# Last third of a down projection by seven products for six of eight blocks, up tiles woven three deep, and adding transfers issued later

## The chip, the cores and the metric

The kernel runs on one core of a Trainium2 chip. The metric is the device time of one execution in microseconds (us): the median of three runs. A further execution was recorded by the hardware profiler; its instruction times, waits and transfers are the trace that the text reads.

## What is computed

One inference step of a hybrid decoder layer for a prompt of 512 tokens and 8 sample tokens with shared weights: mixer, cross attention and a gated feed-forward part, each added to the residual. All numbers are 32-bit floats. The change touches the feed-forward part alone:

```python
def conv_ffn(xn, prefix, w_up, conv_w, conv_b, w_down):
    T = xn.shape[1]
    up = xn @ w_up                                   # 1024 -> 2 x 2816
    ext = jnp.concatenate([prefix, up], axis=1)
    c = conv_b
    for k in range(CONV_W):                          # width 3, causal
        c = c + conv_w[k] * ext[:, k:k + T]
    gate, val = jnp.split(c, 2, axis=-1)
    return (jax.nn.silu(gate) * val) @ w_down, ext[:, -(CONV_W - 1):]
...
    y_ffn, ffn_state = conv_ffn(rmsnorm(h, g_ffn), ffn_prefix, w_up, conv_w, conv_b, w_down)
    return h + y_ffn, pool_state, nsa_state, ffn_state
```

A final rmsnorm over the 1024 channels of `h + y_ffn` follows.

## The kernel before

Channels lie on the 128 partitions, the 520 tokens in two halves `r` of 260 columns (`HT`). There are `KT` = 8 blocks of 128 model channels and `FT` = 22 tiles of 128 hidden channels; an up tile `j` has a gate and a value part (`v` = 0, 1). For precision a weight block W is split into a rounded part `w_hi` (ScalarE copy, L117) and the rest `w_lo` (VectorE subtraction, L120), the moving operand likewise, and a product of two blocks takes three matmuls: hi by hi, hi by lo and lo by hi. A matmul has 260 columns. So one classic block of weights costs six matmuls for both token halves.

**Seven products.** Up tiles `NA` = 7 to 21 go by a Strassen-Winograd scheme (`up_seven`): the gate and value parts against the even and odd blocks of input channels form a 2 by 2 block product with the two token halves, which takes seven half-token products of 4 x 3 = 12 matmuls instead of eight. They are named 1, 5, 2, 6, 3, 7, 4 in the code. Products 1, 6, 7 and 4 go into one half `a` of a PSUM bank, 5 and 3 into its other half `c`, product 2 into a bank `b`. Product 7 adds onto what 6 left in `a`, so `a` has to be read between them. The mixed inputs (`xm4`, `xm3`) are made once by `mixes`. The mixed weights are made per tile: products 5 and 7 need a sum of two blocks of `w_up`, which a DMA from GpSimd's queue adds in memory to a block that has been loaded (L1880, `accum_op`); product 6 needs the block of 1 plus that of 5 (`sum2`) and product 3 the block of 2 plus that sum (`sum4`), which VectorE adds (L120, `tt`).

**The down projection** sums over 22 hidden tiles in three parts (`PARTS`: tiles 0-6, 7-14, 15-21). Each part runs over the 8 output blocks `d`; each group is added to the residual `hT` (L120). Parts 0 and 1 are woven between the up products (`downs`), part 2 comes last: blocks 0 to 3 as steps (`last_down`), blocks 4 to 7 in the tail (L2070), one token half after the other, so that the norm and the stores of half 0 (L2030, L2048, L2052) can run beside half 1.

**The order of the work.** `steps` is a list of steps, each one load (SyncE's queue, `load_unit`), one split (`prep`), the matmuls (`mm`, L1829 for classic, L1890 for the seven) and what follows them (`post`). The loop over `m` issues the load up to `EARLY` = 13 steps ahead, the split `AHEAD` = 3 steps ahead, then the matmuls of step `m`, then `POPS` = 2 pieces of the deferred convolution and gate work (`behind`: `conv`, L1680 to L1684, and `gate`). Loads go to 13 units of raw weights (`w_u`, `raw_x`); splits to a ring of four units (`w_hi`, `w_lo`). A unit is loaded again when the splits and sums that read it are done. A list scheduler of the framework then orders each engine's queue. Every engine works its queue in order. From tile 8 on, a row of the steady pattern is: seven steps of 12 matmuls and one `downs` block of 42 or 48.

Of the kernel before, what the change touches and what calls it, by code (L numbers as in the profile page):

```python
# [9 lines left out]
F32 = mybir.dt.float32  # L10
# [22 lines left out]
FT = DFF // P  # L33
MEM = 256
# [73 lines left out]
def decoder_step(ctx: ExitStack, tc: tile.TileContext, A, O):  # L108
# [1580 lines left out]
    def gate(j):  # L1689
# [6 lines left out]
        yield  # L1696
        tt(g, g, u, OP.mult)
        yield
        if NA <= j < PARTS[2][0]:
            if not hid_mid:  # L1700
                hid_mid.extend(ptile(ab3, [P, KT, 2, HT], t, F32R, name="h_mid") for t in ("x3_hi", "x3_lo"))
            hid[j] = tuple(t[:, j - NA] for t in hid_mid)
        else:
            hid[j] = tuple(ptile(ff, [P, 2, HT], t, F32R, bufs=7) for t in ("h_hi", "h_lo"))
# [25 lines left out]
    NI = KT // 2  # L1730
    xm4 = [ptile(actp, [P, 4, NI, HT], "act_a", F32R, bufs=2, name="xm4") for _ in range(2)]
    xm3 = ptile(ff, [P, 2, 3, NI, HT], "xm3", F32R)
    B11, B21, B22, T3_, N1, N2, T4_ = range(7)
# [25 lines left out]

    mix = mixes()  # L1760
# [28 lines left out]
    class Step:  # L1789

        def __init__(self, mm, load=None, prep=None, post=None, held=False):
            self.load_, self.prep_, self.mm_, self.post_, self.held = load, prep, mm, post, held
# [23 lines left out]

    def classic(ps_of, src, xs, kt, post):

        out = []
        for k0 in range(0, kt, 4):  # L1820
# [11 lines left out]
            out.append(Step(mm, load=lambda k0=k0, n=n: load_unit(rows(src, k0, n), n), post=post if k0 + n == kt else None))  # L1832
# [12 lines left out]
    def up_classic(j):  # L1845
        out = []
        for v in range(2):
# [8 lines left out]
            out.append(classic(ps, w_up[:, up_cols(v, j)], xs3, KT, post))  # L1856
        return out[0] + out[1]

    def down(pi, d, then=None):
# [8 lines left out]
        return classic(ps, w_down[j0 * P:j1 * P, d * P:(d + 1) * P], lambda k: hid[j0 + k], j1 - j0, post)  # L1868

    def up_seven(j):  # L1870

        ac, bb = held("pp"), held("t")

        def block(m, s):
            return w_up[:, up_cols(m, j)].rearrange("(i s p) c -> p s i c", s=2, p=P)[:, s]

        def both(a, b):
            def load():
                u = load_unit(a)
                pool.dma_start(u[1], b, accum_op=OP.add)  # L1880
# [33 lines left out]

        def out21():
            acopy(exts[j][:, 1, 0, 2:], a_of(False), scale=-1.0)
            behind.extend((conv(j, 1), gate(j)))

        s = {}
        s[1] = Step(product(a_of, B11, True), lambda: load_unit(block(0, 0)), held=True)  # L1920
        s[5] = Step(product(c_of, N1, True), both(block(1, 0), block(1, 1)), post=keep, held=True)
        s[2] = Step(product(b_of, B21, True), lambda: load_unit(block(0, 1)), post=out11, held=True)

        def sum2():
            tt(s[1].raw, s[1].raw, s[5].raw, OP.add)
            s[5].free()
            return s[1].raw

        def sum4():
# [244 lines left out]
```

## Time and profile before

| | |
|---|---|
| median of three runs (lowest, highest) | 827.56 us (827.38, 827.99) |
| the profiled execution, by its own time | 827.17 us |
| its span, first to last instruction | 825.5 us |
| mean granted TensorE clock | 0.996 |
| TensorE, VectorE, ScalarE busy share of the span | 98%, 73%, 54% |
| last loads, splits and matmuls of the up and down stage with seven products | 509 to 815 us of the span |

The profile's lines give busy time, count and mean duration of a group; matmuls overlap, so the mean duration of one (285 ns) is longer than the distance from one to the next (about 120 ns), which the chain of waits shows. In the chain, PE is TensorE. DVE is VectorE, ACT ScalarE, POOL GpSimd, SPq SyncE's queue.

### The profile page before, as it was taken

The page shows a single profiled execution, that of the slowest core. Times are in us where ns is not written, and L with a number is a line of the kernel's source. Part 1 is how long each engine was busy: PE and PEld are TensorE (multiplying, and loading weights), DVE is VectorE, ACT ScalarE, POOL GpSimd, SP SyncE. Part 2 cuts the span into 40 slices and gives each one's busy share as a digit, 9 for nine tenths or more (in the row PEclk, how much of TensorE's full clock was granted, in tenths as well). Part 3 has the DMA queues.
Part 4 walks back from the last instruction along what each step waited for, and adds up shares of the span by engine and source line. Part 5 has one row for each costly group of instructions (what it writes and reads, how often), then busy time and mean ns, then how long its engine had stood idle before and what let it go on. Part 6 is the DMA issues. An engine that isn't in the chain of part 4 may idle for free.

```text
span 825.5 us, 17791 instructions
## 1 busy us (share of the span) xinstructions
PE 808.3 (98%) x6891; PEld 753.7 (91%) x6891; DVE 605.2 (73%) x1460; ACT 447.9 (54%) x940; POOL 95.3 (12%) x100
## 2 busy tenths in 40 slices
PE   9999999899999999999999999999999999999996
PEld 8998878877778899999799999999999999999995
DVE  6644686887657776888673799997888887887714
ACT  6741347667665553444343465666666656665541
POOL 2300111000000031000032000111111111100021
PEclk9999999999999999999999999999999999999998
DMA  9988975833222283677443224756866866754422
GB/s 327 304 257 289 411 285 182 270 115 116 77 77 53 64 254 106 202 251 254 137 115 103 77 78 126 154 134 152 165 143 147 168 145 142 160 135 121 171 110 104
DMA packets 146366, 137.87 MB, mean 167 GB/s; under 512 B 6417, under 2 KB 133265, under 8 KB 144089
## 3 DMA queue, kind: packets, MB, share of 16 engines
q1 hardware_dynamic: 127224, 114.63, 44.5%
q0 software_dynamic: 18624, 21.26, 12.0%
q8 instruction: 54, 0.88, 0.4%
q10 hardware_dynamic: 432, 0.84, 0.3%
q14 instruction: 32, 0.25, 0.1%
HBM read 129.56 MB, written 10.69 MB: 170 GB/s over the span
## 4 chain that ended last, share of the span: by engine, by line
PE 90%; DVE 3%; ACT 3%; DMA 2%; issue 1%; SPq 0%; DVEq 0%; ACTq 0%
PE ps_pp L205 29%; PE ps_pp L1890 16%; PE ps_pp L1829 16%; PE ps_t L1890 3%; PE ps_tb L1266 3%; PE ps_o L1155 2%; PE ps_pp L2070 2%; PE ps_tb L1072 2%; PE ps_sc L1108 2%; PE ps_tf L1140 2%; PE ps_x L1467 1%; PE ps_tb L1234 1%; PE ps_x L1488 1%; ACT prob L1118 1%; PE ps_s L1528 1%
## 5 line engine op out<-in xcount | busy, mean ns | idle before, releaser
L1890 PE MATMUL ps_pp<-xm,w_hi 128*128 128x260 f32 x720 | 133.3, 285 | 0.0
L1890 PEld LDWEIGHTS ps_pp<-xm,w_hi 128*128 128x128 f32 x720 | 110.9, 188 | 2.3 <-ACT ext L117 0.2
L117 ACT ACTIVATE w_hi<-w_u 128x512 fp32r<-128x512 f32 (+2 forms) x110 | 72.7, 661 | 66.4 <-PE ps_pp L1890 22.7
L1890 PE MATMUL ps_pp<-xm,w_lo 128*128 128x260 f32 x360 | 101.5, 282 | 0.0
L120 DVE TENSOR_TENSOR w_lo<-w_u,w_hi 128x512 fp32r<-128x512 f32 (+2 forms) x110 | 80.1, 729 | 16.6 <-ACT w_hi L117 15.3
L1890 PEld LDWEIGHTS ps_pp<-xm,w_lo 128*128 128x128 f32 x360 | 67.7, 188 | 0.0
L120 DVE TENSOR_TENSOR hT<-hT,ps_pp 128x520 f32<-128x520 f32 (+1 forms) x44 | 28.4, 645 | 45.0 <-PE ps_pp L205 17.9
L205 PE MATMUL ps_pp<-x_hi,w_hi 128*128 128x260 f32 x288 | 59.9, 286 | 0.0
L205 PE MATMUL ps_pp<-x_hi,w_lo 128*128 128x260 f32 x288 | 59.6, 285 | 0.0
L205 PE MATMUL ps_pp<-x_lo,w_hi 128*128 128x260 f32 x288 | 58.5, 284 | 0.0
L117 ACT ACTIVATE w_hi<-w_raw 128x1024 fp32r<-128x1024 f32 (+1 forms) x38 | 35.1, 922 | 41.3 <-PE ps_pp L205 30.0
L1118 ACT ACTIVATE prob<-prob,mx 128x384 f32<-128x384 f32 (+3 forms) x64 | 35.4, 555 | 19.3 <-DVE mx L1116 19.1
L120 DVE TENSOR_TENSOR w_lo<-w_raw,w_hi 128x1024 fp32r<-128x1024 f32 (+1 forms) x38 | 41.4, 1089 | 6.1 <-ACT w_hi L117 5.8
L205 PEld LDWEIGHTS ps_pp<-x_hi,w_lo 128*128 128x128 f32 x288 | 44.9, 188 | 0.6 <-issue 0.4
L205 PE MATMUL ps_pp<-xn_hi,w_hi 128*128 128x260 f32 x208 | 45.1, 291 | 0.2 <-issue 0.2
L205 PEld LDWEIGHTS ps_pp<-x_hi,w_hi 128*128 128x128 f32 x288 | 44.9, 188 | 0.3
L1880 POOL DMA_DIRECT2D w_u<-in_w_up_dram x19 | 24.4, 1286 | 178.9 <-DMA w_u<-in_w_up_dram 106.8
L205 PEld LDWEIGHTS ps_pp<-x_lo,w_hi 128*128 128x128 f32 x288 | 44.4, 188 | 0.4 <-issue 0.4
L120 DVE TENSOR_TENSOR w_lo<-raw_x,w_hi 128x512 fp32r<-128x512 f32 (+1 forms) x53 | 35.7, 674 | 10.3 <-ACT w_hi L117 9.6
L205 PE MATMUL ps_pp<-xn_lo,w_hi 128*128 128x260 f32 x208 | 42.9, 285 | 0.3 <-DVE xn_lo L129 0.3
L205 PE MATMUL ps_pp<-xn_hi,w_lo 128*128 128x260 f32 x208 | 43.0, 286 | 0.0
L117 ACT ACTIVATE w_hi<-raw_x 128x512 fp32r<-128x512 f32 (+1 forms) x53 | 32.8, 618 | 18.1 <-PE ps_pp L1890 13.1
(495 smaller groups left out, 2309.8 us busy)
## 6 DMA issues: line engine op xcount, KB each, us to landing
w_u<-in_w_up_dram SPq DMA_DIRECT2D x57, 256.0 KB, 3.2
xkr<-in_cache_mem_dram SPq DMA_DIRECT2D x16, 512.0 KB, 4.7
xvr<-in_cache_mem_dram SPq DMA_DIRECT2D x16, 512.0 KB, 7.1
raw_x<-in_w_up_dram SPq DMA_DIRECT2D x26, 256.0 KB, 3.4
Kt<-in_k_t_dram SPq DMA_DIRECT2D x48, 128.0 KB, 3.2
w_u<-in_w_up_dram SPq DMA_DIRECT2D x10, 512.0 KB, 4.3
w_u<-in_w_down_dram SPq DMA_DIRECT2D x20, 256.0 KB, 4.4
w_u<-in_w_up_dram POOLq DMA_DIRECT2D x19, 256.0 KB, 5.8
```

Of the source, the lines that this page charges most:

```text
L117: act.activation(o, i, AF.Copy, scale=scale)
L120: (eng or dve).tensor_tensor(o, a, b, op=op)
L205: pe.matmul(o, a[:, k, :], x[:, hf, :], start=(k == 0 and j == 0), stop=(k == kt - 1 and j == 2))
L1072: pe.matmul(ps[:, :HT], a[:, k, :], y[x][:, k, hf, :], start=(k + j == 0), stop=(k == 3 and j == 2))
L1108: pe.matmul(ss_[hl][:, 0:n], Qst[:, h, qc], k[:, g, u, 0:n], start=(u == 0), stop=(u == 1), skip_group_check=True)
L1118: act.activation(p[:, 0:nk], p[:, 0:nk], AF.Exp, bias=mx[:, hh:hh + 1], scale=-1.0, accum_out=sm[:, hh:hh + 1])
L1140: pe.transpose(pt[:, hh * P:(hh + 1) * P], pr[hh][:, kb * P:(kb + 1) * P], ident)
L1155: pe.matmul(po[hp * 64:(hp + 1) * 64, g * 256:(g + 1) * 256], Vtok[:, br, kb, g * 64:(g + 1) * 64], pTs[kb][:, hp * 256:(hp + 1) * 256], s ...
L1266: pe.matmul(ps[i], x[:, k, ts_], w[:, kl, :], start=(k == 0 and j == 0), stop=(k == KT - 1 and j == 2))
L1829: pe.matmul(ps[:, hf, :HT], a[:, k, :], x[:, hf, :], start=(k0 + k + j == 0), stop=(k0 + k == kt - 1 and j == 2))
L1880: pool.dma_start(u[1], b, accum_op=OP.add)
L1890: pe.matmul(ps, a[:, i, :], b, start=(first and i + q == 0), stop=(i == NI - 1 and q == 2), skip_group_check=True)
```

## The change

1. **Part 2 of the down projection by seven products.** `PARTS` becomes tiles 0-6, 7-13 and 14-21, so the last part has eight hidden tiles. `DOWN_ORDER` puts its even tiles ahead of its odd ones. Output blocks 0 to 5 go in three pairs through `down_seven`; blocks 6 and 7 stay classic in the tail (`D0` = 6). The gated values of tiles 14 to 21 are kept unsplit (`raw_hid`) and `hidden_mixes` makes the mixed and split operands from them (`hx_b`, `hx_m`, `hx_e`) while the last five `downs` blocks run. Sums of weights for these three groups are made by VectorE.
2. **Up tiles woven three deep** (`weave`): a row is 6 of tile s, 1 of t, 4 of the tile before s, 3 of s, a `downs` block in rows 0 to 7 alone, 5 and 2 of t, 7 of s. Rows 8 to 13 have no `downs` block; the last row takes three. `sum2` and `sum4` of tiles 8 to 21 become adding DMAs from one raw unit to another on GpSimd's queue (`dma`), issued right after the splits of products 5 and 2.
3. **Adding transfers later:** the adding DMAs of products 5 and 7 are issued `LATER` = 5 steps after their load, or when their split comes within four steps, not with the load. What is read of `a` and `c` after product 2 now includes the copy that followed product 5 before (`out11`). Posts get high priority; `POPS` is 3.
4. **Layouts:** `w_up` and `w_down` are laid out so that a partition's part of a block lies in one row of 2 KB (before: rows of 512 bytes).
5. **Tail:** the weights of blocks 6 and 7 are split beside the last four steps, and the norm and stores of half 0 stand at fixed places of half 1 (`lead`, `issue_after`).

```diff
@@
+PARTS = ((0, 7), (7, 14), (14, FT))
+DOWN_ORDER = list(range(14)) + list(range(14, FT, 2)) + list(range(15, FT, 2))
...
+        if j >= NB2:
+            if not raw_hid:
+                raw_hid.append(ptile(ff, [P, KT, 2, HT], "hA", name="raw_hid"))
+            tt(raw_hid[0][:, j - NB2], g, u, OP.mult)
...
+    def hidden_mixes():
...
+        for i in range(NI):
+            e, o = raw_hid[0][:, 2 * i], raw_hid[0][:, 2 * i + 1]
+            both = raw_hid[0][:, 2 * i:2 * i + 2].rearrange("p s r t -> p r s t")
+            at_ = [t[:, :, i].rearrange("p (r s) t -> p r s t", r=2) for t in blk]
+            acopy(at_[0], both)
+            n, t = (ptile(ff, [P, 2, HT], "cv", bufs=3, name="hz") for _ in range(2))
+            tt(n[:, 0], e[:, 0], e[:, 1], OP.subtract)
+            tt(t[:, 0], o[:, 1], e[:, 1], OP.subtract)
+            dve.scalar_tensor_tensor(n[:, 1], n[:, 0], -1.0, o[:, 1], op0=OP.mult, op1=OP.subtract)
+            acopy(mid[:, 0, 2, i], t[:, 0])
+            dve.scalar_tensor_tensor(t[:, 1], n[:, 1], -1.0, o[:, 0], op0=OP.mult, op1=OP.subtract)
+            acopy(mid[:, 0, 0:2, i], n)
+            tt(at_[1], both, at_[0].bitcast(F32), OP.subtract)
+            acopy(end[:, 0, i], t[:, 1])
+            tt(mid[:, 1, 0:2, i], n, mid[:, 0, 0:2, i].bitcast(F32), OP.subtract)
+            tt(mid[:, 1, 2, i], t[:, 0], mid[:, 0, 2, i].bitcast(F32), OP.subtract)
+            tt(end[:, 1, i], t[:, 1], end[:, 0, i].bitcast(F32), OP.subtract)
...
+    LATER = 5
+    adds = []
+
+    def seven(block, mixed, ac, bb, posts, dma):
...
                 u = load_unit(a)
-                pool.dma_start(u[1], b, accum_op=OP.add)
+                adds.append([LATER, u[1], b])
...
+        def add(o, a):
+            if dma:
+                pool.dma_start(s[o].raw, s[a].raw, accum_op=OP.add)
+            else:
+                tt(s[o].raw, s[o].raw, s[a].raw, OP.add)
 
         def sum2():
-            tt(s[1].raw, s[1].raw, s[5].raw, OP.add)
             s[5].free()
             return s[1].raw
 
         def sum4():
-            tt(s[2].raw, s[2].raw, s[1].raw, OP.add)
...
+    def weave(rows, places, last):
+        prev = None
+        for n, s in enumerate(rows):
+            t = rows[n + 1] if n + 1 < len(rows) else None
+            seq = ([s[6], t[1]] if prev and t else [t[1], s[6]] if t else [s[6]]) + ([prev[4]] if prev else [])
+            if t:
+                seq += [s[3]] + (downs.pop(0) if n in places else []) + [t[5], t[2], s[7]]
+            else:
+                seq += last() + [s[3]] + last() + [s[7]] + last() + [s[4]]
+            steps.extend(seq)
+            prev = s
+
+    weave(sevens, (0, 1, 2, 3, 4, 5, 6, 7), lambda: downs.pop(0))
...
-    D0 = 4
-    for d in range(D0):
-        steps += last_down(d)
+    D0 = 6
+    groups = [down_seven(q, down_done) for q in range(D0 // 2)]
+    steps += [groups[0][i] for i in (1, 5, 2)]
+    weave(groups, (), lambda: [])
...
-    AHEAD, EARLY, POPS = 3, 13, 2
+    AHEAD, EARLY, POPS = 3, 13, 3
...
+        soon = [s.raw for s in steps[max(m + AHEAD, 0):m + AHEAD + 4] if hasattr(s, "raw")]
+        for e in list(adds):
+            e[0] -= 1
+            if e[0] <= 0 or any(e[1] is r for r in soon):
+                adds.remove(e)
+                pool.dma_start(e[1], e[2], accum_op=OP.add)
```

Where sums of weights are made shows in the queues. In these rows `w_u` and `raw_x` are raw units, `in_w_up` is the matrix in memory. GpSimd's queue before, five rows of the steady pattern:

```order
L1880 DMA w_u_5885<-in_w_up_dram 128x4x128 [waits DMAHW5_49,DMASW1_49]
L1880 DMA raw_x_5483<-in_w_up_dram 128x4x128 [waits DMAHW3_49,DMASW2_49,DVE_49]
L1880 DMA w_u_5884<-in_w_up_dram 128x4x128 [waits DMAHW4_49,DMASW3_49]
L1880 DMA w_u_5885<-in_w_up_dram 128x4x128 [waits DMAHW2_49,DMASW4_49,DVE_49]
L1880 DMA w_u_5885<-in_w_up_dram 128x4x128 [waits DMAHW3_49,DMASW5_49]
```

Each row adds a block from memory to a loaded unit, two per tile, and nothing else stands between them.

GpSimd's queue in the changed kernel, tiles 19 to 21 in the rows without a `downs` block:

```order
L1966 DMA raw_x_5483<-raw_x_5483 128x512 [waits DVE_49,Activation_49]
L1966 DMA raw_x_5483<-raw_x_5483 128x512 [waits DMASW4_49,DMAHW6_49,DMASW3_49,DVE_49]
L2115 DMA raw_x_5483<-in_w_up_t_dram 128x512 [waits DMAHW4_49,DMASW5_49]
L1966 DMA w_u_5885<-w_u_5885 128x512 [waits DMASW6_49,DVE_49,Activation_49]
L1966 DMA w_u_5885<-w_u_5885 128x512 [waits DMAHW3_49,DMASW6_49,DVE_49]
L2115 DMA w_u_5885<-in_w_up_t_dram 128x512 [waits DMAHW3_49,DMASW0_49]
L1966 DMA w_u_5884<-w_u_5884 128x512 [waits DMASW2_49,DMASW1_49,DMAHW1_49,DVE_49,Activation_49]
L1966 DMA raw_x_5483<-w_u_5884 128x512 [waits DMAHW0_49,DMASW1_49,DVE_49]
```

The adds of loaded blocks (L2115, L1880 before) stay; each tile gains a pair of adds from unit to unit (L1966), the second of which waits for the first to land.

VectorE's queue before, around the two sums of one tile (`w_lo` rows are splits, the rows with two raw units are `sum4` and `sum2`):

```order
L120 TENSOR_TENSOR raw_x_5483<-raw_x_5483,w_u_5885 128x512
L120 TENSOR_TENSOR hT_2321<-hT_2321,ps_pp_7482 128x520 [waits PE_49]
L120 TENSOR_TENSOR w_lo_5889<-w_u_5885,w_hi_5888 128x512 [waits DMAHW2_49,Activation_49]
L1913 SCALAR_TENSOR_TENSOR ext0_5890<-ps_pp_7372,ext0_5890 128x260 [waits PE_49]
L120 TENSOR_TENSOR w_lo_5887<-w_u_5885,w_hi_5886 128x512 [waits DMAHW3_49,Activation_49]
L120 TENSOR_TENSOR w_u_5885<-w_u_5885,raw_x_5483 128x512 [waits DVE_49]
```

Each sum stands just ahead of the split that reads it, or one or two places earlier, in the same queue.

VectorE's queue in the changed kernel, a row without a `downs` block; the five rows are the splits of 4 (tile 18), 3 (tile 19), 5 and 2 (tile 20) and 7 (tile 19):

```order
L122 TENSOR_TENSOR w_lo_5887<-w_u_5885,w_hi_5886 128x512 [waits DMAHW0_49,Activation_49]
L122 TENSOR_TENSOR w_lo_5887<-raw_x_5483,w_hi_5886 128x512 [waits DMASW4_49,Activation_49]
L122 TENSOR_TENSOR w_lo_5889<-w_u_5885,w_hi_5888 128x512 [waits DMASW6_49,PE_49,Activation_49]
L122 TENSOR_TENSOR w_lo_5889<-w_u_5885,w_hi_5888 128x512 [waits DVE_49,DMAHW3_49,PE_49,Activation_49]
L122 TENSOR_TENSOR w_lo_5887<-w_u_5884,w_hi_5886 128x512 [waits DMASW1_49,PE_49,Activation_49]
```

The sums are gone from VectorE's queue; the split of 3 now waits for a transfer (DMASW), and the split of the next tile's 5 stands behind it.

TensorE's queue before, the end of product 6 (`xm3`), four rows of a `downs` block (`h_hi`, `h_lo`), the start of product 7 (`xm4`) on the same bank 8104:

```order
L1890 MATMUL ps_pp_8104<-xm3_6066,w_hi_5886 128x260 x2
L1890 MATMUL ps_pp_8104<-xm3_6066,w_lo_5887 128x260
L1829 MATMUL ps_pp_8214<-h_hi_6060,w_hi_5888 128x260 x2
L1829 MATMUL ps_pp_8214<-h_lo_6061,w_hi_5888 128x260 x2
L1829 MATMUL ps_pp_8214<-h_hi_6060,w_lo_5889 128x260 x2
L1829 MATMUL ps_pp_8214<-h_hi_6189,w_hi_5888 128x260 x2
L1890 MATMUL ps_pp_8104<-xm4_6064,w_hi_5886 128x260
```

Product 7 adds to what 6 left in bank 8104, with eight matmuls of bank 8214 between them.

TensorE's queue in the changed kernel, the end of product 6 on the bank 8654 (`xm3`) in a row without a `downs` block, and the start of what follows it, product 1 of the next tile on the bank 8785:

```order
L1955 MATMUL ps_pp_8654<-xm3_6066,w_hi_5888 128x260 x2
L1955 MATMUL ps_pp_8654<-xm3_6066,w_lo_5889 128x260
L1955 MATMUL ps_pp_8785<-xm4_6064,w_hi_5886 128x260
L1955 MATMUL ps_pp_8785<-xm4_6065,w_hi_5886 128x260
L1955 MATMUL ps_pp_8785<-xm4_6064,w_lo_5887 128x260
```

After 1 come 4 of the tile before, 3 of this tile, 5 and 2 of the next, and then 7 on bank 8654: five products stand between 6 and 7, where eight matmuls stood.

More of the change, by code (lines that the diff above doesn't have):

```diff
@@ L1703, in gate @@
         else:
-            hid[j] = tuple(ptile(ff, [P, 2, HT], t, F32R, bufs=7) for t in ("h_hi", "h_lo"))
+            if not hid_ends:
+                end_tiles()
+            hid[j] = tuple(t[:, j] for t in hid_ends)
         acopy(hid[j][0], g)
@@ L1805, in prep @@
             raw = self.prep_() if self.prep_ else self.raw
+            assert all(o is not raw for _, o, _ in adds)
             if self.load_ and not self.held:
@@ L1810, in prep @@
             split(self.w[0], self.w[1], raw)
+            if self.after:
+                self.after()
         def mm(self):
@@ L1830, in mm @@
                                       stop=(k0 + k == kt - 1 and j == 2))
-            out.append(Step(mm, load=lambda k0=k0, n=n: load_unit(rows(src, k0, n), n), post=post if k0 + n == kt else None))
+            out.append(Step(mm, load=lambda k0=k0, n=n: load_unit(src[:, k0:k0 + n], n), post=post if k0 + n == kt else None))
         return out
@@ L1990, in decoder_step, with tail_split @@
     loaded = 0
+    wl = []
+    def tail_split(u):
+        if u in tail_done:
+            return
+        tail_done.add(u)
+        if not wl:
+            wl.extend(ptile(ab3, [P, KT, 2, HT], t, F32R, name="wl").rearrange("p a r t -> p (a r t)")
+                      [:, 0:(KT - D0) * kt * P].rearrange("p (d k c) -> p d k c", k=kt, c=P) for t in ("x3_hi", "x3_lo"))
+        dl, k0 = u // 2, u % 2 * 4
+        split(*(t[:, dl, k0:k0 + 4] for t in wl), tail_raw[u].raw)
+    tail_done = set()
+    hidden = hidden_mixes()
+    kept = [(O["win_keep"].rearrange("b t c g d -> b t (c g d)"), A["cache_win"][0, :, 1:WIN].rearrange("b t c g d -> b t (c g d)")),
+            (O["pool_keep"], A["state_pool"][0, :, 1:15, :]), (O["ffn_keep"], A["state_ffn"][0, :, 1, :])]
     for m in range(-AHEAD, len(steps)):
@@ L2003, in decoder_step @@
             continue
+        if loaded == len(loads) and not adds and kept:
+            for o, i in kept:
+                with last_on(EN.SP):
+                    sp.dma_start(o, i)
+            kept = ()
         for _ in range(2 + (m < 2)):
             next(mix, None)
+        if m >= ups_end:
+            for _ in range(4):
+                next(hidden, None)
+        if m >= len(steps) - 4 and hasattr(tail_raw[-1], "raw"):
+            tail_split(m - len(steps) + 4)
         steps[m].mm()
@@ L2015, in decoder_step @@
         run(g)
-    assert loaded == len(loads)
-    wl_hi, wl_lo = (ptile(ab3, [P, KT, 2, HT], t, F32R, name="wl").rearrange("p a r t -> p (a r t)")
-                    [:, 0:(KT - D0) * kt * P].rearrange("p (d k c) -> p d k c", k=kt, c=P) for t in ("x3_hi", "x3_lo"))
+    assert loaded == len(loads) and not adds
+    for u in range(2 * (KT - D0)):
+        tail_split(u)
+    wl_hi, wl_lo = wl
     eps_d = ptile(ff, [P, 1], "eps_d")
@@ L2056, in decoder_step @@
     stores = iter(())
+    lead = None
     for hf in range(2):
```

198 lines of the change are left out of this document (113 added, 85 removed).

## Prediction

> **What bounds the kernel now.** First the page's busy shares, then the stretches of the stage that changes, from the two last classic up tiles (509.2 us) to the end. Columns: length, then busy time of TensorE's matmuls, its weight loads, VectorE, ScalarE, GpSimd, then granted clock, DMA share, GB/s.
>
> ```profile
> PE 808.3 (98%) x6891; PEld 753.7 (91%) x6891; DVE 605.2 (73%) x1460; ACT 447.9 (54%) x940; POOL 95.3 (12%) x100
> ```
>
> ```profile
> 509.20:532.30 23.10, 23.10 (x195) 23.10 (x194) 22.72 (x41) 14.31 (x29) 5.16 (x4) 1.00 0.72 158
> 674.00:759.00 85.00, 85.00 (x703) 84.29 (x703) 69.83 (x123) 52.12 (x106) 9.01 (x7) 1.00 0.62 142
> 767.30:793.20 25.90, 25.90 (x218) 25.90 (x218) 13.79 (x24) 13.14 (x28) 4.43 (x4) 1.00 0.50 197
> 793.20:815.20 22.00, 22.00 (x186) 21.97 (x186) 7.22 (x16) 8.85 (x20) 5.77 (x7) 1.00 0.17 69
> 815.20:825.50 10.30, 2.19 (x14) 1.64 (x13) 3.51 (x8) 1.08 (x3) 0.00 (x0) 0.65 0.26 103
> ```
>
> TensorE is busy throughout until 815 us, at full clock, even where VectorE is busy for 22.72 of 23.10 us. So time goes only if matmuls go, or gaps too small for this view. The chain of waits shows those (start, length, what):
>
> ```profile
> 561.10 1.45 PE ps_t L1890 x12
> 562.55 1.45 PE ps_pp L1890 x12
> 564.00 0.95 PE ps_pp L1829 x8
> 564.95 1.63 PE ps_pp L1890 x12
> 566.58 4.09 PE ps_pp L1829 x34
> ...
> 767.29 25.89 PE ps_pp L1829 x216
> 793.18 12.70 PE ps_pp L2070 x105
> 805.89 1.24 PE ps_t L2030 x12
> 807.12 1.90 PE ps_pp L2070 x15
> 809.02 0.36 PE ps_t L2048 x3
> 809.38 5.76 PE ps_pp L2070 x48
> ```
>
> One matmul costs TensorE 25.89 / 216 = 0.120 us, so a product of 12 costs 1.44. Product 7 (the 12 after the eight of the `downs` block) takes 1.63: it waits 0.18 for the read of what 6 left in its bank.
>
> **Removed: matmuls.** Parts 1 and 2 had 8 x 48 + 8 x 42 = 720 matmuls. Now part 1 has 8 x 42 = 336, the three pairs 3 x 7 x 12 = 252, blocks 6 and 7 2 x 48 = 96: 684. 36 x 0.120 = **-4.3 us**, on the path since nothing else is late there. The up tiles keep their number.
>
> **Removed: the gap before product 7.** It stands in the 14 rows of the weave: 14 x 0.18 = **-2.6 us**. Five products (7.2 us) now lie between 6 and 7. 4 follows 7 by two products (2.9 us) for one short read on VectorE, 6 follows 2 by one (1.44 us) for ScalarE's copy of 520 columns; what could be late is that copy, see the rivals.
>
> **Tail.** The four tail blocks took 168 x 0.120 = 20.1 us of 21.96; of the other 1.8, 1.24 is twelve one-column matmuls (0.1 each, less a wait for a square) and 0.36 transposes. Both come again. The norm of half 0 now stands 12 matmuls (1.44 us) behind the last group of that half, and the transposes 15 (1.8 us) behind the norm, about what its chain takes. I take **-0.5** (bounds -1.2, 0). Behind the last product the chain is the same 10.3 us; half 0's three multiplications now lie just ahead of the last add, beside 21 matmuls (2.5 us).
>
> **Added: two adds from unit to unit per tile, tiles 8 to 21.** 28 sums leave VectorE for GpSimd's queue, which waits in it: the second add of a tile waits there until the first lands, and with it whatever is queued behind, the adds of loaded blocks. Their nearest rows are those blocks' adds (L1880) and a plain transfer of 220 KB in 128 rows (L1973):
>
> ```profile
> L1880 POOL DMA_DIRECT2D w_u<-in_w_up_dram x19: 1274/1283/1328, 509.5 to 718.4; - x19
> DMA to landing us min/median/max: 4.5/5.9/7.3
> ```
>
> ```profile
> L1973 POOL DMA_DIRECT2D out_ffn_t_dram<-last x1: 595/595/595, 769.1 to 769.1; - x1
> DMA to landing us min/median/max: 2.6/2.6/2.6
> ```
>
> And what transfers take of the 16 DMA engines, from 500 us on (326 us; q1 loads, q0 adds; packets, MB, share), with the page's first slices, where long rows come at full load:
>
> ```profile
> q1 hardware_dynamic: 64104, 37.39, 39.1%
> q0 software_dynamic: 15376, 7.83, 19.1%
> ```
>
> ```profile
> DMA  9988975833222283677443224756866866754422
> GB/s 327 304 257 289 411 285 182 270 115 116 77 77 53 64 254 106 202 251 254 137 115 103 77 78 126 154 134 152 165 143 147 168 145 142 160 135 121 171 110 104
> ```
>
> An add of 0.262 MB takes all engines for 0.191 x 326 x 0.262 / 7.83 = 2.1 us, a load in long rows 262 / 327 = 0.8. Let A be the time from a split's end to an add's landing. With 128 rows GpSimd issues in 0.6 instead of 1.28 us, and if the data cost two loads (1.6) another 0.5 goes: the least and the median become 3.3 and 4.7. I take A = 4.0; outer bounds are 2.6 (L1973) and 5.9 (median unchanged).
>
> The Trainium skill ("Collectives: The Full Stack", "The bandwidth ceiling") says that an adding transfer is slow because it reads two sources, not because it adds. By it an add costs two loads, 1.6 us; by bytes of the row above it stays 2.1. No row here has an add in rows of 2 KB; A would be 4.0 or 4.5, and the forecast the same or 2.0 later.
>
> The two halves of a split, from 509 us on:
>
> ```profile
> L117 ACT ACTIVATE w_hi<-w_u 128x512 fp32r<-128x512 f32 (+1 forms) x97 | 60.2, 622 | 42.6 <-PE ps_pp L1890 22.7 <-PE ps_pp L1829 13.0 <-ACT ext L117 2.9
> L120 DVE TENSOR_TENSOR w_lo<-w_u,w_hi 128x512 fp32r<-128x512 f32 (+1 forms) x97 | 65.9, 680 | 16.3 <-ACT w_hi L117 15.0
> ```
>
> Where a row has a `downs` block it lasts 126 x 0.120 = 15.1 us; there is room. Rows 8 to 13 last only 84 x 0.120 = 10.1 us. Their chain: first add lands after A, second after 2A, then the split of 3 (hi 0.62, lo 0.69) and behind it in both queues the split of the next tile's 5 (0.7), which starts the next pair: a row needs 2A + 2.1. At A = 4.0 that is 10.1, just covered. Splits run three steps ahead (4.3 us, less 1.3 for the split: 3.0 of cover for the whole stretch). I put **+1.0** (bounds 0 for A under 4; at 4.7, 6 x (11.5 - 10.1) - 3.0 = 5.4).
>
> **Adds of loaded blocks, later.** Loads run about nine steps ahead in these rows (13 us), the add five steps on, so 5.8 us are left for an A of 4: nothing, unless GpSimd's queue stands still. The loads keep their number and size; their rows in memory get four times as long, which only shortens them.
>
> **Added: VectorE's work.** Further groups of it, 509.2 to 767 us (busy, mean ns, idle before):
>
> ```profile
> L1684 DVE SCALAR_TENSOR_TENSOR cv<-ext,taps,cv 128x512 f32<-128x512 f32 x35 | 26.1, 746 | 0.0
> L120 DVE TENSOR_TENSOR cv<-cv 128x520 f32<-128x520 f32 x17 | 11.8, 693 | 0.0
> L120 DVE TENSOR_TENSOR ext<-ext,ps_pp 128x260 f32<-128x260 f32 x15 | 6.4, 425 | 6.6 <-PE ps_pp L1890 6.6
> L120 DVE TENSOR_TENSOR cv<-cv,base 128x8 f32<-128x8 f32 x34 | 5.7, 167 | 0.0
> L120 DVE TENSOR_TENSOR xm<-raw_x,xm 128x1040 fp32r<-128x1040 f32 x1 | 1.2, 1232 | 0.0
> ```
>
> A row without a block holds 7 splits, 4 convolution steps, 2 small adds, one gate product, 3 reads of PSUM: 4.8 + 3.0 + 0.3 + 0.7 + 1.3 = 10.1 us of instructions for 10.1 us. They overlap: the first stretch above kept up at 98%. The last row and five blocks (8 x 42 + 60 matmuls, 47.5 us) hold 46 us: 24 splits and sums 15.4, eight adds 5.5, four of `hidden_mixes` at 6 x 0.43 + 0.69 + 1.23 = 4.5 each, the rest 7. The three groups: 7 splits, 2 sums, 7 adds, 9.2 us of 10.1. All fits, narrowly: **+1.0** for both (bounds 0, 4).
>
> **Sum.** 825.5 - 4.3 - 2.6 - 0.5 + 1.0 + 1.0 = 820.1 us of span; 827.17 - 825.5 = 1.7 around it: 821.8, against 827.17. The median lies 0.4 above the profiled execution, so the forecast is **822.2 us**.
>
> **Rivals.**
> - *All hidden.* No stall anywhere and the tail at its bound: 827.6 - 4.3 - 2.6 - 1.2 = 819.5. For it: TensorE never waited at VectorE's 98%. Against: three queues get tight at once. Chance 0.20.
> - *The chain of adds sets the pace (slower).* Rows 8 to 13, from A = 4.9 on (6 x (11.9 - 10.1) - 3.0 = 7.8 eats the gain of 7.4 and more). At A = 5.2 (the median less only GpSimd's 0.7): 6 x 2.4 - 3.0 = 11.4, 832.6 us. For it: 5.9 was the median with only 0.62 to 0.72 DMA share. Against: shorter issue, less data time. Chance 0.11.
> - *The DMA engines are full.* A row without a block moves five loads and four adds: 5 x 0.8 + 4 x 2.1 = 12.4 us of engine time for 10.1; 6 x 2.3 - 3.0 = 10.8, 832 us. With adds at 1.6 it is 10.4 and hardly shows. Chance 0.06. The Trainium skill ("DMA: Bandwidth & Descriptors", "Issuing engines are not separate DMA queues") speaks against the change here: transfers of SyncE and GpSimd share the same 16 engines. The trace bears it out: L1880 spreads from 4.5 to 7.3 us beside loads.
> - *VectorE falls behind beside `hidden_mixes`* (46 of 47.5 us): 4 us more, 826. Chance 0.08.
>
> **The numbers.** Forecast 0.55 (820 to 825.5). About 0.2% (1.7 us) is what a measurement of this kernel can tell from no change. Faster: 0.55 + 0.20 = 0.75; the case beside `hidden_mixes` counts as within: 0.08; slower 0.11 + 0.06 = 0.17. The range reaches from the best case to where the slower ones begin to settle: 819 to 831.
>
> **What would show it.** Right: in the chain of waits, products of 12 at 1.44 us in the rows without a block, no 1.63; 684 matmuls in the down parts counted; L1966 landing in about 4 us; VectorE about 90% in those rows. Wrong: ScalarE's `w_hi` waiting for adds (L1966) by more than 2 us a row with TensorE gaps behind it; DMA share near 1 there; gaps between the last blocks and the first group.

## The result, and the profile after

The changed kernel takes 835.09 us (median of 6 runs, 833.98 to 839.0) beside 827.77 us of the kernel before (6 runs, 827.25 to 828.87): a ratio of 1.0092, 95% interval 1.0073 to 1.0110. The forecast was 822.2 us, its range ended at 831.

The profiled execution took 837.29 us, with a span of 835.6 against 825.5. The feed-forward stage, from its first classic matmul on, is 325.6 us long instead of 316.4; what lies ahead of it took 0.9 us more. The stage's start varies from 506.2 to 512.6 us between the profiled executions below.

The busy shares: 36 matmuls fewer, as foreseen; GpSimd busier by the 28 adds from unit to unit and by six adds of loaded blocks for the three groups of the down projection (L2115 has 36 adds, L1880 had 30).

```profile
PE 805.9 (96%) x6855; PEld 751.3 (90%) x6855; DVE 609.0 (73%) x1484; ACT 454.7 (54%) x955; POOL 112.2 (13%) x132
```

The stretches of the stage: rows with a `downs` block (540 to 655), rows 8 to 13 with the start of the last row (655 to 736), a piece of these at half clock, the five blocks, and what follows the last product. Columns as in the prediction: length, TensorE's matmuls, weight loads, VectorE, ScalarE, GpSimd, granted clock, DMA share, GB/s.

```profile
540.00:655.00 115.00, 115.00 (x959) 114.88 (x958) 84.19 (x153) 70.63 (x146) 28.31 (x33) 1.00 0.81 187
655.00:736.00 81.00, 69.76 (x546) 68.52 (x545) 58.83 (x112) 49.48 (x111) 18.35 (x21) 0.96 0.77 172
672.50:675.90 3.40, 3.40 (x18) 3.40 (x17) 3.30 (x7) 1.93 (x5) 1.78 (x2) 0.50 0.38 94
736.00:781.00 45.00, 45.00 (x378) 45.00 (x377) 39.74 (x76) 24.80 (x48) 4.86 (x6) 1.00 0.63 159
825.80:835.60 9.80, 1.87 (x14) 1.49 (x13) 3.55 (x8) 1.08 (x3) 0.00 (x0) 0.69 0.49 191
```

Rows with a block keep TensorE full, and so do the five blocks beside `hidden_mixes`. In rows 8 to 13 it is busy for 69.8 of 81.0 us. VectorE (58.8 of 81.0 us, 0.73) and ScalarE (0.61) are no busier there than in the rows with a block, and the DMA engines are a little less busy (0.77). On the mean nothing is saturated; something waits in a circle. In two stretches of 3.41 us the clock is halved as well (third row; the other starts at 686.1).

Who waits, from the view of waits after 505 us (total, times, longest):

```profile
POOL w_u L2115 <- DMA w_u<-in_w_up_t_dram: 50.5, 14, 8.2
PE ps_pp L1955 <- ACT ext L119: 11.1, 5, 3.6
ACT w_hi L119 <- DMA raw_x<-w_u: 7.6, 4, 4.2
ACT w_hi L119 <- DMA w_u<-in_w_up_t_dram: 6.9, 3, 3.8
ACT w_hi L119 <- DMA w_u<-raw_x: 5.7, 2, 4.4
```

TensorE waits 11.1 us for ScalarE's copies `ext` (12.2 us when counted from matmul to matmul, less 0.120). Those copies hardly wait for anything of their own (0.27 us in the two gaps below): they stand in ScalarE's queue behind a `w_hi` that waits for an add to land. The lines of L1966, the sums from unit to unit, and of L2115, the adds of loaded blocks, have the landings (the second and fourth row):

```profile
  ACT w_hi L119: 23.2, 12
DMA to landing us min/median/max: 3.4/4.9/8.4
...
  ACT w_hi L119: 6.9, 3
DMA to landing us min/median/max: 4.0/5.5/7.6
```

The timeline of two of the gaps (start, length, engine, line; rows of VectorE and TensorE left out) shows the circle:

```profile
668.63 0.63 ACT L119 ACTIVATE w_hi<-w_u 128x512 fp32r<-128x512 f32 x1 [4.35 <-DMA w_u<-raw_x]
668.67 0.80 SPq L1849 DMA_DIRECT2D raw_x<-in_w_up_t_dram  x2
669.11 0.86 POOL L1966 DMA_DIRECT2D raw_x<-w_u  x1 [3.95 <-DMA w_u<-raw_x]
...
673.94 0.33 SPq L1849 DMA_DIRECT2D w_u<-in_w_up_t_dram  x1
673.97 0.63 ACT L119 ACTIVATE w_hi<-raw_x 128x512 fp32r<-128x512 f32 x1 [1.48 <-DMA raw_x<-w_u]
674.00 0.89 POOL L2115 DMA_DIRECT2D raw_x<-in_w_up_t_dram  x1 [4.03 <-issue]
...
674.57 1.12 SPq L1849 DMA_DIRECT2D raw_x<-in_w_up_t_dram  x2
674.60 1.18 POOL L1966 DMA_DIRECT2D raw_x<-w_u  x1
...
683.61 0.80 SPq L1849 DMA_DIRECT2D w_u<-in_w_up_t_dram  x2
683.64 0.63 ACT L119 ACTIVATE w_hi<-raw_x 128x512 fp32r<-128x512 f32 x1 [4.21 <-DMA raw_x<-w_u]
684.08 0.86 POOL L1966 DMA_DIRECT2D w_u<-raw_x  x1 [8.29 <-issue]
```

One landing lets a split run (668.63, 673.97, 683.64). With it units come free, and within 1 us SyncE issues two or three loads and GpSimd one or two adds. At 674 these are two adds and three loads at once, and the second add's reader starts 9.0 us after its issue (674.60 to 683.64). Between the bursts hardly a transfer is left to run, and within them the DMA engines are full, with adds and loads mixed (columns as above; the next to last is the DMA share, which passes 1.00 where packets overlap):

```profile
678.00:680.00 2.00, 2.00 (x19) 2.00 (x18) 1.67 (x3) 1.40 (x5) 0.00 (x0) 1.00 0.99 223
682.00:684.50 2.50, 1.30 (x11) 1.09 (x10) 0.20 (x1) 0.86 (x2) 0.42 (x1) 1.00 0.06 11
685.00:689.00 4.00, 2.57 (x12) 2.57 (x13) 4.00 (x9) 1.94 (x5) 1.96 (x3) 0.64 1.05 239
707.50:710.00 2.50, 0.74 (x7) 0.54 (x5) 0.31 (x1) 0.97 (x2) 0.54 (x1) 1.00 0.12 21
```

So the mean of 0.77 is made of full bursts and of empty pauses between them.

What transfers take of the engines, from 500 us on (336 us), and the page's slices of the DMA engines:

```profile
q1 hardware_dynamic: 18968, 38.24, 35.8%
q0 software_dynamic: 9280, 17.01, 30.7%
```

```profile
DMA  9988965833212383677233324677888867866453
```

An add of 0.262 MB now costs the 16 engines 0.307 x 336 x 0.262 / 17.01 = 1.59 us, a load 0.358 x 336 x 0.262 / 38.24 = 0.82. A row without a block asks 5 x 0.82 + 4 x 1.59 = 10.5 us of them and lasts 10.1; a row with one asks 2 loads more (one is short: 1.4 us), 11.9 us of 15.1 or 0.79, about the 0.81 that the first stretch shows.

### The profile page after: what moved, and what is told of

It is laid out like the page before. It is cut to its first block, busy times and chain, and to the rows that moved or that the text cites. A ratio compares the mean times of both kernels' runs of the same rounds, so it can differ in the third digit from the quotient of the medians.

```text
span 835.6 us, 17898 instructions
## 1 busy us (share of the span) xinstructions
PE 805.9 (96%) x6855; PEld 751.3 (90%) x6855; DVE 609.0 (73%) x1484; ACT 454.7 (54%) x955; POOL 112.2 (13%) x132
## 5 line engine op out<-in xcount | busy, mean ns | idle before, releaser
L1955 PE MATMUL ps_pp<-xm,w_hi 128*128 128x260 f32 x720 | 134.4, 287 | 11.2 <-ACT ext L119 11.1
L1955 PEld LDWEIGHTS ps_pp<-xm,w_hi 128*128 128x128 f32 x720 | 113.5, 192 | 12.6 <-ACT ext L119 12.1
L119 ACT ACTIVATE w_hi<-w_u 128x512 fp32r<-128x512 f32 (+2 forms) x117 | 75.8, 653 | 79.5 <-PE ps_pp L207 21.4
L122 DVE TENSOR_TENSOR w_lo<-w_u,w_hi 128x512 fp32r<-128x512 f32 (+2 forms) x117 | 84.7, 729 | 27.5 <-ACT w_hi L119 26.7
L1955 PE MATMUL ps_pp<-xm,w_lo 128*128 128x260 f32 x360 | 103.2, 287 | 0.0
L122 DVE TENSOR_TENSOR hT<-hT,ps_pp 128x520 f32<-128x520 f32 (+1 forms) x54 | 31.1, 583 | 30.2 <-PE ps_pp L207 17.7
L122 DVE TENSOR_TENSOR w_lo<-raw_x,w_hi 128x512 fp32r<-128x512 f32 (+1 forms) x59 | 40.0, 688 | 17.6 <-ACT w_hi L119 17.3
L119 ACT ACTIVATE w_hi<-raw_x 128x512 fp32r<-128x512 f32 (+1 forms) x59 | 36.0, 619 | 27.7 <-DMA raw_x<-w_u 7.6
L1896 PE MATMUL ps_pp<-h_mid,w_hi 128*128 128x260 f32 x224 | 36.0, 282 | 0.0
```

The source lines that it names most:

```text
L119: act.activation(o, i, AF.Copy, scale=scale)
L122: (eng or dve).tensor_tensor(o, a, b, op=op)
L1896: pe.matmul(ps[:, hf, :HT], a[:, k, :], x[:, hf, :], start=(k0 + k + j == 0), stop=(k0 + k == kt - 1 and j == 2))
L1955: pe.matmul(ps, a[:, i, :], b, start=(first and i + q == 0), stop=(i == NI - 1 and q == 2), skip_group_check=True)
```

## The experiments

Each ratio is to the kernel before on the same chip, with its 95% interval; the runs are from several chips, so that kernels are best compared by their ratios. "Wait" is TensorE's idle time in rows 8 to 13 and at their borders, from the view of waits between 640 and 745 us; "ask" is the engine time of a row's transfers, worked out with 0.82 and 1.59 (0.53 for an add of a quarter: e5_quarter's adds take 0.236 of 320 us, the 36 others 0.191 of 318 in e3_vector, the difference over 28), over its 10.1 us.

| kernel | ask of rows 8 to 13 | units | wait, us | median us | ratio |
|---|---|---|---|---|---|
| changed kernel | 1.04 | 13 | 11.1 | 835.09 | 1.0092 (1.0073 to 1.0110) |
| e1_spread | 0.89 over six rows | 13 | 6.4 | 831.32 | 1.0059 (1.0043 to 1.0075) |
| e2_pair | 1.04 | 13 | 9.8 | 833.96 | 1.0085 (1.0062 to 1.0109) |
| e3_vector | 0.72 | 13 | 0 | 819.87 | 0.9925 (0.9907 to 0.9943) |
| e4_noboth | 0.72 | 13 | 0 | 819.90 | 0.9929 (0.9909 to 0.9949) |
| e5_quarter | 0.83 | 13 | 1.0 | 823.00 | 0.9963 (0.9943 to 0.9983) |
| e6_one | 0.88 | 13 | 1.2 | 822.70 | 0.9954 (0.9939 to 0.9970) |
| e8_copy | 0.72 and the copy | 13 | 2.8 | 824.98 | 0.9994 (0.9980 to 1.0009) |
| e9_split | 0.72 | 13 | 1.6 | 821.15 | 0.9936 (0.9923 to 0.9950) |
| e10_late_rows | 1.04 | 13 | 6.8 | 831.89 | 1.0044 (1.0024 to 1.0064) |
| e11_units12 | 1.04 | 12 | 15.7 | 846.65 | 1.0225 (1.0204 to 1.0245) |
| e12_cv2 | 1.04 | 13 | 10.2 | 837.49 | 1.0123 (1.0085 to 1.0162) |
| e13_units14 | 1.04 | 14 | 2.9 | 834.39 | 1.0065 (1.0042 to 1.0087) |
| e14_units14b | 1.04 | 14 | 2.5 | 830.59 | 1.0037 (1.0024 to 1.0051) |
| e15_vector12 | 0.72 | 12 | 0 | 826.07 | 0.9989 (0.9977 to 1.0001) |

**A block in every second row.** My first theory (C) was the rival of the prediction: two adds, one behind the other, set the pace. D was the engines' volume, Q GpSimd's queue.

```diff
-    weave(sevens, (0, 1, 2, 3, 4, 5, 6, 7), lambda: downs.pop(0))
+    weave(sevens, (0, 1, 2, 3, 4, 5, 6, 7, 9, 11, 13), lambda: [])
```

> Edit: the three `downs` blocks of the last row stand in rows 9, 11 and 13 instead, the last row has none; the same 64 adding transfers, the same products. Theory C (the chain of two adds in rows 8 to 13 sets the pace): in the changed kernel the landings of those adds were late, ScalarE's queue waited for them, and TensorE stood still for 12.2 us in six places, behind which the granted clock was halved for 2 x 3.4 us (3.4 us lost). A row with a block lasts 15.1 us and has room for 2A + 2.1 up to A = 6.5, so every second row catches up: gaps under 1 us in all, no half clock before the tail, 837.3 (the profiled execution) less 15.6, so 820 to 823. Theory D (the 16 DMA engines are full in rows without a block, 10.4 us of transfers for 10.1): rows 8, 10 and 12 are still full, 3 x 0.3 is no stall by itself, the time falls to 822 to 826 with gaps left in these rows. Theory Q (GpSimd's queue stands in order whatever the row's length): no change, 833 to 836.

831.32 us, 3.8 below the changed kernel (2.7 by the ratios), where C expected 12 to 15, and waits of 6.4 us in the profiled execution (which, at 826.62, was the fastest of its six). That is too much for C, and for D as stated. It fits a limit on the volume of which only 0.8 can be had: three rows of 10.5 and three of 11.9 us ask 67.2 us of 75.6; at 0.8 they need 84, 8.4 more, less the 3.0 of cover. The 0.8 is read from the trace here, not derived.

**The second add freed from the first.**

```diff
-        s[2] = Step(product(b_of, B21, True), lambda: load_unit(block(0, 1)), post=posts[2], held=True, after=lambda: add(2, 1))
+        s[2] = Step(product(b_of, B21, True), lambda: load_unit(block(0, 1)), post=posts[2], held=True, after=lambda: add(2, 5))
```

> Edit: the second add of a tile takes unit 5 (loaded) instead of unit 1 (just summed), so that it no longer waits for the first; as many transfers of the same size. It leaves the first term out of the weights of product 3. Theory C (two adds one behind the other): a row needs A + 2.1, 7 to 9 us of 10.1, the gaps go, 820 to 823. Theory D (DMA engines full): the volume is unchanged, the gaps stay, 832 to 836, and both adds land late. Theory Q (GpSimd's queue in order: adds of loaded blocks and of the pair wait for each other): the second add no longer blocks the queue for the first's landing, most of the gaps go, 822 to 826.

833.96 us: no change worth the name, waits of 9.8 us. C falls. The adds no longer queue behind each other, and land no sooner:

```profile
  ACT w_hi L119: 17.1, 7
DMA to landing us min/median/max: 3.4/5.1/8.8
```

**The sums back on VectorE.**

```diff
-        return seven(lambda m, s: w_up[m, j, :, s], xm, ac, bb, posts, j > NA)
+        return seven(lambda m, s: w_up[m, j, :, s], xm, ac, bb, posts, False)
```

> Edit: the 28 sums from unit to unit are made on VectorE again, as before the change; the new row order, the seven products of the last third and the later adds stay. Theory C: the chain of adds is gone; VectorE takes 28 x 0.7 = 19.6 us more, 1.4 us in a row. Rows with a block have room (15.1 us). Rows 8 to 13 hold 10.1 + 1.4 = 11.5 us of VectorE work for 10.1 if none of it overlaps, 6 x 1.4 less 3 us of cover = 5.4 us at most: 821 to 828, no half clock. If VectorE overlaps as in the stretch before the weave (98% busy without a gap), 820 to 823. Theory V (VectorE is the real bound, and moving the sums off it is what the change lives on): slower than the changed kernel, over 836.

819.87 us, faster than both kernels, the version to keep. The chain of waits runs through the rows without a block with no gap at all, 8.62 + 1.45 = 10.07 us each:

```profile
653.89 8.62 PE ps_pp L1955 x72
662.52 1.45 PE ps_t L1955 x12
663.97 8.62 PE ps_pp L1955 x72
672.59 1.45 PE ps_t L1955 x12
...
718.66 5.03 PE ps_pp L1896 x42
723.69 1.44 PE ps_pp L1955 x12
```

VectorE makes 28 sums more than in the changed kernel and is busy 0.96 of the time in the rows without a block, and TensorE doesn't notice:

```profile
655.00:720.00 65.00, 65.00 (x544) 65.00 (x544) 62.68 (x119) 50.16 (x110) 7.30 (x9) 1.00 0.66 166
```

**Fewer adds, with the chained pair kept.**

```diff
-                adds.append([LATER, u[1], b])
+                if keep:
+                    adds.append([LATER, u[1], b])
...
-        return seven(lambda m, s: w_up[m, j, :, s], xm, ac, bb, posts, j > NA)
+        return seven(lambda m, s: w_up[m, j, :, s], xm, ac, bb, posts, j > NA, j < 15)
```

> Edit: for up tiles 15 to 21 the second block is not added to the two units that hold a difference or sum of two blocks (the 14 adds from memory are left out), so that GpSimd's queue holds only the chained pair there. It leaves those blocks out of the weights of products 5 and 7. Theory C with A stretched by what else is in flight: the pair's landing falls from a median of 4.9 (up to 8.4) to 3.4 to 4.5 us, a row needs 2 x 4 + 2.1 = 10.1 to 11: gaps of 0 to 3 us in all, 820 to 825. Theory C with A fixed by the transfer itself: the landing stays at 4.9, 6 x (11.9 - 10.1) - 3 = 8 us of gaps, 828 to 831. Theory D: a row moves 5 x 0.8 + 2 x 1.6 = 7.2 us of engine time for 10.1, no gap, 820 to 823, at any landing time.

819.90 us. The pair is still chained and still transfers; with 7.3 us of transfers instead of 10.5 in a row TensorE waits for nothing. The pair's adds land in 4.5 us at the median between 640 and 720 us; by the chain's sum a row would need 2 x 4.5 + 2.1 = 11.1 us, and it keeps to 10.1. After this and e2_pair the chain by itself is out of the question. Whether bytes or queue entries do it was open.

**As many entries, fewer bytes.**

```diff
-                pool.dma_start(s[o].raw, s[a].raw, accum_op=OP.add)
+                pool.dma_start(s[o].raw[:, 0:1], s[a].raw[:, 0:1], accum_op=OP.add)
```

> Edit: each of the 28 adding transfers from unit to unit moves only the first of the unit's four blocks (128 x 128, 64 KB instead of 256); as many entries in GpSimd's queue, the same waits, the same units held for as long. It leaves three quarters of those sums out of the weights of products 3 and 6. What has fallen: two adds one behind the other as the whole cause (with the second freed from the first the time stayed at 834). Theory B (bytes in flight: one landing releases a split, that frees units, loads start beside the next two adds, and all of them share the 16 engines, so that an add lands after 7 to 9 us instead of 3.4): a row moves 5 x 0.8 + 2 x 1.6 + 2 x 0.4 = 8 us of engine time, the adds land in 2.5 to 4 us, no gap over 0.5 us, 819 to 823. Theory Q (the queue itself: entries that wait in order on GpSimd and units held until a landing, whatever their bytes): the gaps of 12 us stay for the most part, 829 to 836.

823.00 us, waits of 1.0: by the ratios about three quarters of what e3_vector gains come back, with the same entries and the same order of waits. So most of it is bytes, not the queue. The smaller adds also land earlier (3.9 us at the median in these rows, 4.9 in the changed kernel), so this run alone doesn't part the bytes from the landing time; e2_pair and e4_noboth speak for the bytes.

**One add a tile instead of two.**

```diff
-            if dma:
+            if dma and o == 2:
```

> Edit: the first sum of a tile is made on VectorE, the second alone by an adding transfer; the result is the same. Theory B: a row moves 5 x 0.8 + 3 x 1.6 = 8.8 us of engine time for 10.1 and waits once, not twice, for a landing: gaps of 0 to 3 us in all, 820 to 824. Theory Q: three entries a row instead of four, and a pair no longer stands behind itself: about half of the 12 us stays, 825 to 830. VectorE as the limit: 10.8 us of work in rows of 10.1, at most 6 x 0.7 less 3 of cover = 1.2 us more than either.

822.70 us and waits of 1.2, as theory B had it.

**Foreign bytes beside the good version.**

```diff
-        return seven(lambda m, s: w_up[m, j, :, s], xm, ac, bb, posts, j > NA)
+        return seven(lambda m, s: w_up[m, j, :, s], xm, ac, bb, posts, False)
...
+        if m == row_at[8]:
+            o, i = kept.pop(0)
+            with last_on(EN.Activation):
+                act.dma_start(o, i)
```

> Edit: the sums on VectorE as in e3_vector (819.9 there), and the copy of 4.2 MB from memory to memory, which stands at the end of SyncE's queue, is issued on ScalarE's at the start of row 8. It puts foreign bytes beside the rows without a block and nothing into GpSimd's queue; no unit waits for it. Theory B: to the 5 x 0.8 + 2 x 1.6 = 7.2 us of a row come some 13 us of copy while it runs, the engines are full for two to three rows, loads and adds from memory land late there (over 7 us), gaps of 3 to 10 us: 823 to 830. Theory Q: nothing waits in order for it, 819 to 821.

824.98 us, some 5 us more than without the copy, about as B had it: TensorE waits 2.6 us for a `w_hi`, which itself waits 5.2 us for a transfer from memory (view of waits), and one stretch of half clock follows. With a stream that no unit holds back, the engines are kept busier than 0.8; the stretch beside the copy:

```profile
690.00:700.00 10.00, 10.00 (x86) 10.00 (x85) 9.96 (x20) 7.85 (x18) 1.72 (x2) 1.00 1.06 261
```

So 0.8 is not the engines' own ceiling; the full bursts of the changed kernel say the same for adds and loads together.

**Adds only where rows are long, and only where they are short.** `NA < j <= 15` in place of `j > NA`, and `j > 15`:

> Edit: sums by adding transfers for tiles 8 to 15 alone, whose sums fall in rows with a block; on VectorE for tiles 16 to 21, whose sums fall in rows 8 to 13. Theories B and Q alike: rows of 15.1 us have room for four adds, rows of 10.1 us have only the two of the loaded blocks left: no gap over 0.5 us before the tail, as with all sums on VectorE, 819 to 822. If the adds in rows with a block cost something that shows only later (units that come free late and loads that start late), 823 to 830.

> Edit: sums by adding transfers for tiles 16 to 21 alone (rows 8 to 13), on VectorE for tiles 8 to 15; the mirror of e9_split. Theory B as it now stands: by the runs so far an adding transfer takes 1.6 us and a load 0.8 us of the 16 engines; rows 8 to 13 ask 5 x 0.8 + 4 x 1.6 = 10.4 us of engine time, and where such rows ran they kept the engines busy 0.8 of the time, so each takes 13 us instead of 10.1: 6 x 2.9 less 3 of cover = 14 us over the 820 of the versions without gaps: 831 to 835, though the rows before are free of the sums. If the gaps were made up in the rows before (units held back there): 820 to 824.

821.15 and 831.89 us. The adds cost about nothing in rows with a block (one wait of 1.6 us at the border, behind a `w_hi` that waited 4.6 us for a transfer from memory), and most in the rows without: by the ratios 0.0119 of the 0.0167 between e3_vector and the changed kernel. The two parts add up to 0.0130; the rest shows only when both are there, and no run says why.

**Fewer and more units.** Why 0.8? A unit is held from the issue of its load until the last add that reads it has landed, and a load starts when a unit is free. So the ring may set how much is under way. `(raw_x, 5)` becomes `(raw_x, 4)`:

> Edit: 12 raw units instead of 13; else the changed kernel. Theory U (loads start only when a unit comes free, a unit is held until an add that waits for another landing, so the ring of units keeps the engines from being busy more than 0.8 of the time): 12/13 of the share, 0.74, a row without a block takes 14.1 us instead of 13.0, 6 more in all, and rows with a block ask 7 x 0.8 + 4 x 1.6 = 12.0 us, 16.2 us at 0.74, over their 15.1: 840 to 850. Theory E (0.8 is what the engines themselves reach with adds and loads mixed): nothing changes, 833 to 837.

846.65 us, in U's range of 840 to 850 and far from E. But U had also expected the rows with a block to grow to 16.2 us at a share of 0.74, and they did not: TensorE never waits there, and the engines are as busy as with 13 units (0.83; 0.81 in the changed kernel).

```profile
540.00:655.00 115.00, 115.00 (x959) 114.87 (x958) 86.09 (x157) 72.33 (x150) 27.66 (x32) 1.00 0.83 191
```

For 14 units the tile `raw_x` gets 6 blocks, and the convolution's tile one buffer less; e12_cv2 is the control:

> Edit: two buffers instead of three for the convolution's tile, 13 raw units; the control for e13_units14, which needs that room. Both theories: 0 to 3 us more than the changed kernel, 833 to 838, since a convolution may wait for the gate of the one before.

> Edit: 14 raw units, loads up to 14 steps ahead, two buffers for the convolution's tile as in e12_cv2, with which it is compared. Theory U: 14/13 of the share, 0.86; a row without a block takes 12.1 us instead of 13.0, 5 us less than e12_cv2. Theory E: the same time as e12_cv2 within 1 us.

> Edit: 14 raw units as in e13_units14, but loads at most 13 steps ahead (with 14, the first load into that tile came before the mixes were done with it), two buffers for the convolution's tile as in e12_cv2 (837.5, with gaps of 11.6 us in rows 8 to 13). Theory U (ring of units times landing sets how busy the engines get): share 0.80 x 14/13 = 0.86 in those rows, gaps of 3 to 7 us there, 4 to 8 us less than e12_cv2, 829 to 834. Theory E (the engines' own ceiling at 0.8): gaps of 10 to 13 us as before, 836 to 839.

In e13_units14 the early load leaves wrong weights in the first product that uses that unit; every engine executes as many instructions as in e14_units14b. It is 3.1 us faster than its control, where U expected 5 and E at most 1. The stretch from 655 to 735 us, with 12 (e11_units12), 13 (e12_cv2) and 14 units (e14_units14b):

```profile
655.00:735.00 80.00, 64.26 (x482) 63.42 (x481) 49.81 (x94) 43.48 (x96) 17.49 (x21) 0.91 0.71 159
```

```profile
655.00:735.00 80.00, 69.77 (x528) 68.57 (x527) 54.52 (x105) 46.93 (x106) 18.25 (x21) 0.91 0.76 170
```

```profile
655.00:735.00 80.00, 77.43 (x631) 75.93 (x630) 63.45 (x120) 52.85 (x118) 18.80 (x23) 1.00 0.84 195
```

The DMA share is 0.71, 0.76 and 0.84, and TensorE waits 15.7, 10.2 and 2.5 us. So in the rows without a block the ring sets how much is under way (U), not the engines (E). The share is near 0.06 per unit, but that is a rough figure: the changed kernel, e2_pair and e10_late_rows, with 13 units too, have 0.77, 0.80 and 0.80 in the same stretch. Nor does it hold for other rows: with 12 units the rows with a block reached 0.83. What 12 units can carry depends on how long each is held; the loads of a `downs` block are not held for a sum, which would explain the difference, but no run tests it. The times are 846.65, 837.49 and 830.59 us; the last has 2.5 us of other waits in the tail, for GpSimd's part of the norm (`acc`) and a split, and a stretch of half clock there.

> Edit: the sums on VectorE as in e3_vector (819.9), with 12 raw units instead of 13; with the sums as transfers 12 units cost 11.5 us (846.7). Theory U: without the sums a unit is not held for two landings and a row asks 5 x 0.8 + 2 x 1.6 = 7.2 us of the engines, 0.71 of its time, below the 0.74 that 12 units give: no gaps before the tail, 819 to 822. If 12 units are too few whatever the sums do (loads late for everyone): 825 to 835.

The rows are free of waits, as U said: 12 units are enough where the sums don't hold them. The time was not as expected, 826.07 us, in the range of the other case: the last groups and the tail wait 3.9 us in all for VectorE and for splits (view of waits after 745 us), and a stretch of half clock follows. So 12 units are too few at the end, whatever the sums do.

## Why the prediction was wrong, step by step

- **Matmuls, -4.3: right.** 6855 instead of 6891.
- **The gap before product 7, -2.6: right.** In the rows of the weave no 1.63 is left; in those with a block, and in e3_vector in all, products take 1.44 (8.62 for six).
- **Tail, -0.5: the number by luck.** The half microsecond was put ahead of the last product, and nothing went there: the twelve one-column matmuls take 1.23 us (1.24 before), the three transposes 0.33 (0.36). It came behind the last product, where the prediction had the same 10.3 us: 9.8 are left. The three terms together are -7.4 us; the feed-forward stage of e3_vector lasts 309.3 us against 316.4 before: -7.1.
- **VectorE's work, +1.0: too much.** It was about 0, though narrow: at 0.96 busy TensorE still didn't wait. That the sums had to leave VectorE was wrong too: with them there the kernel is 1.7% faster (0.9925 against 1.0092).
- **Two adds from unit to unit, +1.0: here it failed.** Rows 8 to 13 cost 12.2 us of gaps and 2 x 1.5 us of half clock, 15.2 of the 16.3 us by which the stage is longer than e3_vector's. The step took A = 4.0 as a property of one add and asked whether 2A + 2.1 fits the row. From issue to landing it was 4.9 at the median and up to 8.4. But the size of A is not the whole error: with 4.9 the step gives 7.8 us instead of 1.0, or 829 in all, still within the range. Of the signs of being wrong, the first came, `w_hi` waiting for these adds by 21.6 us in rows 8 to 13, 3.6 a row; a DMA share near 1 did not (0.77). Yet the chain was not what counted, since without it (e2_pair) the time stayed. A is what comes out of bytes under way together, and the sum that mattered stood in the rival of the DMA engines, with units that are held until an add lands: 5 loads and 4 adds against the length of the row.
- **That rival, 0.06 at 832: the nearest account, its time partly luck.** It weighed the right volume against the right rows, but held the engines to be full, which they are only in bursts. Its add of 2.1 us came from rows of 512 bytes; in rows of 2 KB it is 1.59. The Trainium skill ("Collectives: The Full Stack", "The bandwidth ceiling"), which speaks of the adds of a collective, gave two source reads, so two loads or 1.6 by my estimate, and the trace agrees (2 x 0.82 = 1.64). But then I wrote that at 10.4 of 10.1 us it "hardly shows", as if the engines could be filled to the last packet. They were filled to about 0.8 on the mean: 10.5 / 0.8 = 13.1 us a row, 6 x 3.0 less the 3.0 of cover = 15 us; 12.2 + 3.0 were lost. That sum is made afterwards, with a share read from such rows (0.77 here would give 18), and proves nothing by itself. Too dear an add and engines that fill to the last packet are errors of opposite sign, so 832 came out near 835.
- **"Adds of loaded blocks, later: nothing, unless GpSimd's queue stands still": half right.** The queue did wait (50.5 us for loads), but that is no sign of a loss: in e3_vector it waits 96.7 us for the same loads, with no gap on TensorE. Here it follows loads that started late for want of units. With `LATER = 1` instead of 5 the order of instructions is the same on every engine, so that this part of the change does nothing by itself.
- **The range.** It was built around A, and its upper end, 831, left out the case in which adds, loads and units hold each other up, because each of the three was priced alone.

What stays open: why one landing frees work for so many transfers at once, and so whether another order of loads could smooth the bursts with 13 units, was not tried. Nor is it shown why 12 units are enough for rows with a block, at a share of 0.83, and 13 too few for rows without one when the sums are transfers.

## What to carry to other kernels

Work that is moved from a busy engine to transfers must be weighed per stretch, in DMA engine time against the length of that stretch, and not only by whether one transfer lands in time. If the transfers hold ring buffers, the share that can be reached may be set by the buffers, not by the engines (about 0.8 with 13 buffers in the short rows here): count how many are held, and for how long. A mean share below 1 doesn't say that the engines are free; look whether it is bursts and pauses. And before moving work off an engine because it is 90% busy, look whether anybody waits for it: at 96% nobody did.

## What the runs showed of the hardware

- **Half clock behind a gap.** After a gap of TensorE the granted clock fell to 0.50 for 3.41 or 6.83 us, and matmuls started every 0.217 us instead of 0.120: 1.5 us lost per stretch of 3.41. In the feed-forward stage of all these profiles, up to the last product, it followed nine of ten gaps above 3 us, seven of eleven between 2.0 and 2.9 us, and none of those below that stand alone (gaps counted from matmul to matmul, less 0.120). The Trainium skill ("TensorE: Matmul & The Clock Gate", "HAM oscillation — how this bites in real kernels") asks for no idle gaps over some 3.4 us. The gaps that were enough were often shorter here (seven were under 3 us), and one of 3.74 us was not enough, so a stall should be priced with a likely half clock behind it from 2 us on.
- **Issuing an add.** With 128 rows GpSimd's share is 0.86 us (1.28 before), where I had put 0.6.
